# TensorE's loop over single batches with register addresses, and GpSimd instead of SyncE as the engine that opens and closes the section

## The chip, the cores and the metric

One core of one Trainium2 chip. The metric is the device time of one execution in microseconds; lower is better. The span of a profile runs from the first to the last instruction and is about 2.1 us shorter than the time. "The fifteenth" and "the sixteenth" below are DMA engines in the order in which they finish their share of a transfer. A landing is the moment at which such a share has arrived. A turn is the place in the queue where a store follows loads; a long load packet is one that took more than the usual 1.82 us.

## The reference

```python
batch, m, k, n = 16, 512, 768, 1024          # x: [16, 768, 512], y: [16, 768, 1024], float32
def reference(x, y):
    return np.einsum('bkm,bkn->bmn', x, y).astype(np.float32)
```

## The kernel before

SyncE issues all transfers on one queue. VectorE casts x and y of a batch to bf16, GpSimd turns the casts into counts for TensorE, TensorE does 48 matmuls of 128x128 by 128x512 per batch into two PSUM tensors, ScalarE copies each half out, and a store of 2 MiB follows. The program has buffers for the loads of two batches and for five outputs.

```python
ctx.enter_context(tc.tile_critical())                      # SyncE opens and closes
xb = [ec(nc.sbuf_tensor(f"xb{i}", [P, KT, M], BF16)) for i in range(2)]
yb = [ec(nc.sbuf_tensor(f"yb{i}", [P, KT, N], BF16)) for i in range(2)]
# ...
def parts(b):                                              # y is cast in two parts in these batches
    return 2 if b in (0, 1, 2, 14, 15) else 1
# ...
for b in range(B):                                         # SyncE
    if b >= 2: nc.sync.wait_ge(cast, nx[b - 2])
    wide_dma("x", ...)                                     # 1.5 MiB
    if b >= 2: nc.sync.wait_ge(cast, nx[b - 2] + parts(b - 2))
    wide_dma("y", ...)                                     # 3 MiB
    if b >= LAG: store(b - LAG)                            # 2 MiB, LAG = 4
for b in range(B - LAG, B):
    store(b)
# ...
def batch(i):                                              # TensorE; i is a Python constant
    # ...
    nc.tensor.wait_ge(ready, 2).then_inc(ready, -2)
    for g in range(2):
        nc.tensor.wait_ge(room, 1).then_inc(room, -1)
        for m in range(HB):
            for nt in range(NT):
                for kt in range(KT):
                    if g == 0 and m == 0 and nt == 0 and kt == KH:
                        nc.tensor.wait_ge(ready, 1).then_inc(ready, -1)
                    mm = nc.tensor.matmul(ps[g][:, m, nt], x_w[:, kt, g * HB + m],
                                          yb[i][:, kt, nt * NF:(nt + 1) * NF], ...)
        mm.then_inc(groups, 1)

with nc.Fori(0, B // 2, engines=OrderedEngineSet([pe])):   # a hardware loop, two batches each
    batch(0)
    batch(1)
```

## Time and profile before

| | before |
|---|---|
| time, median of 3 runs | 262.86 us (262.63 to 263.0) |
| span of the profile | 260.7 us |
| DMA queue busy, share of 16 engines | 97.9% |
| TensorE busy | 72%, granted clock 0.91 |
| packets of kind "instruction" | 1, of 16,384 bytes |

The page and the answers of the profile on which the argument rests are in the prediction below. Beside them it uses the trace's records of single DMA packets (start, duration, size) and of landings. The trace has 16 landings for each of the 48 transfers (768), one from each of the 16 DMA engines, and whoever waits for a transfer waits for the last of them: of the last y the fifteenth landed at 233.15 us and the sixteenth at 235.23, and its cast began at 235.26. The packet of 16,384 bytes of kind "instruction" is called the fetch below.

### The profile page before, as it was taken

The numbers are of one execution on the slowest core, as the hardware profiler recorded it, in microseconds if no ns is written. First come the engines' busy times: TensorE is split into PE (matmuls) and PEld (weight loads), VectorE is DVE, ScalarE is ACT, GpSimd is POOL, SyncE is SP. The second block draws the span as 40 slices with busy tenths as digits, with TensorE's granted clock in tenths as the row PEclk, the third lists the DMA queues.
The fourth block names the chain that finished last, engine by engine and source line by source line (L and its number), as shares of the span: only waits on it lengthen the run. The fifth ranks groups of instructions, "written<-read, shape, count | busy, mean of one in ns | idle before, by whom it ended". The sixth has DMA issues, their size and how long they took to land. (4 is left out here: it accounts for less than half of the span.)

```text
span 260.7 us, 1850 instructions
## 1 busy us (share of the span) xinstructions
PE 188.3 (72%) x760; PEld 88.9 (34%) x768; DVE 82.3 (32%) x37; ACT 61.1 (23%) x33; POOL 0.2 (0%) x4
## 2 busy tenths in 40 slices
PE   0049999797955949779695894969869196895930
PEld 0014555343522514324242341434334043341510
DVE  0271743425213252322524114252132523225000
ACT  1001322414230220402223022130412214022220
POOL 0000000000000000000000000000000000000000
PEclk9999999999997997959899796797999889797995
DMA  7998999989999999999999989999898999989984
GB/s 272 422 513 370 475 387 453 430 334 460 425 417 463 400 450 460 420 407 415 473 407 430 473 375 468 392 480 430 380 493 380 470 437 435 422 385 432 435 359 209
DMA packets 4513, 109.07 MB, mean 418 GB/s; under 512 B 768, under 2 KB 768, under 8 KB 768
## 3 DMA queue, kind: packets, MB, share of 16 engines
q1 hardware_dynamic: 4512, 109.05, 97.9%
q8 instruction: 1, 0.02, 0.0%
HBM read 75.50 MB, written 33.55 MB: 418 GB/s over the span
## 5 line engine op out<-in xcount | busy, mean ns | idle before, releaser
L143 PE MATMUL ps<-yb,xb 128*128 128x512 bf16 x760 | 188.3, 410 | 61.4 <-PEq L137 59.3
L143 PEld LDWEIGHTS ps<-yb,xb 128*128 128x128 bf16 x768 | 88.9, 117 | 160.4 <-issue 95.0
L161 ACT COPY ob<-ps 128x2048 f32<-128x2048 f32 x32 | 59.8, 1869 | 189.6 <-PE ps L143 189.6
L124 DVE CAST yb<-ys 128x6144 bf16<-128x6144 f32 (+1 forms) x21 | 54.1, 2596 | 88.0 <-DMA ys<-in_y_dram 88.0
L120 DVE CAST xb<-xs 128x3072 bf16<-128x3072 f32 x16 | 28.2, 1760 | 68.4 <-DMA xs<-in_x_dram 67.2
L161 ACT ACT_TABLE_LOAD x1 | 1.3, 1283 | 1.0 <-SPq L45 1.0
L185 POOL MEMSET const-bfloat16-1.0<- 128x1 bf16 x1 | 0.1, 102 | 0.0
L185 POOL MEMSET const-uint8-127<- 128x1 uint8 x1 | 0.1, 101 | 0.0
L185 POOL MEMSET const-float32-0.0<- 128x1 f32 x1 | 0.1, 99 | 0.2 <-issue 0.2
L185 POOL MEMSET const-float32-1.0<- 128x1 f32 x1 | 0.1, 98 | 0.0
## 6 DMA issues: line engine op xcount, KB each, us to landing
ys<-in_y_dram SPq DMA_DIRECT2D x16, 3072.0 KB, 28.2
out_dram<-ob SPq DMA_DIRECT2D x16, 2048.0 KB, 32.6
xs<-in_x_dram SPq DMA_DIRECT2D x16, 1536.0 KB, 29.7
```

Source lines behind the costliest of these rows:

```text
L120: nc.vector.tensor_copy(xb[i][:], xs[i][:]).then_inc(cast, 1)
L124: nc.vector.tensor_copy(yb[i][:, ks], ys[i][:, ks]).then_inc(cast, 1)
L143: mm = nc.tensor.matmul(ps[g][:, m, nt], x_w[:, kt, g * HB + m], yb[i][:, kt, nt * NF:(nt + 1) * NF], start=(kt == 0), stop=(kt == KT - 1))
L161: cp = nc.scalar.copy(ob[b % NO][:, g * HB:(g + 1) * HB].rearrange("p m (t f) -> p m t f", f=NF), ps[g][:])
L185: nc = _bacc.Bacc("TRN2", target_bir_lowering=False, num_devices=1)
```

## The change

TensorE's loop runs over single batches, an inner hardware loop gives the slot (0 or 1) as a register, and the operands' addresses are computed from it. For that the two slots of xb and yb become one tile each. The order becomes kt outside nt. y is cast in two parts in the last batch only. GpSimd opens and closes the section and waits for the stores at the end. The intent, as far as the code tells it: a shorter program, on TensorE above all.

```diff
-    ctx.enter_context(tc.tile_critical())
+    ctx.enter_context(tc.tile_critical(sync_engine=nc.gpsimd.engine))
-    xb = [ec(nc.sbuf_tensor(f"xb{i}", [P, KT, M], BF16)) for i in range(2)]
-    yb = [ec(nc.sbuf_tensor(f"yb{i}", [P, KT, N], BF16)) for i in range(2)]
+    xb = ec(nc.sbuf_tensor("xb", [P, 2, KT, M], BF16))
+    yb = ec(nc.sbuf_tensor("yb", [P, 2, KT, N], BF16))
     ... (VectorE's casts write xb[:, i] and yb[:, i, ks] accordingly)
-        return 2 if b in (0, 1, 2, 14, 15) else 1
+        return 2 if b in (15,) else 1
-    def batch(i): ... (above)
-    with nc.Fori(0, B // 2, engines=OrderedEngineSet([pe])):
-        batch(0)
-        batch(1)
+    x_w = xb[:].rearrange("p s k (j mo) -> p s k mo j", mo=MT)
+    pe = OrderedEngineSet([nc.tensor.engine])
+    with nc.Fori(0, B // 2, engines=pe):
+        with nc.Fori(0, 2, engines=pe) as s:
+            nc.tensor.wait_ge(ready, 2).then_inc(ready, -2)
+            for mo in range(MT):
+                g, m = divmod(mo, HB)
+                if m == 0:
+                    nc.tensor.wait_ge(room, 1).then_inc(room, -1)
+                for kt in range(KT):
+                    if mo == 0 and kt == KH:
+                        nc.tensor.wait_ge(ready, 1).then_inc(ready, -1)
+                    for nt in range(NT):
+                        mm = nc.tensor.matmul(
+                            ps[g][:, m, nt], x_w[:, bass.ds(s, 1), kt, mo],
+                            yb[:, bass.ds(s, 1), kt, nt * NF:(nt + 1) * NF],
+                            start=(kt == 0), stop=(kt == KT - 1))
+                if m == HB - 1:
+                    mm.then_inc(groups, 1)
     for i in range(NO):
-        nc.sync.wait_ge(so[i], 16 * len(range(i, B, NO)))
+        nc.gpsimd.wait_ge(so[i], 16 * len(range(i, B, NO)))
```

More of the change, by code (lines that the diff above doesn't have):

```diff
@@ L119 @@
         nc.vector.wait_ge(sx[i], n)
-        nc.vector.tensor_copy(xb[i][:], xs[i][:]).then_inc(cast, 1)
+        nc.vector.tensor_copy(xb[:, i], xs[i][:]).then_inc(cast, 1)
         nc.vector.wait_ge(sy[i], n)
@@ L123 @@
             ks = slice(h * KT // parts(b), (h + 1) * KT // parts(b))
-            nc.vector.tensor_copy(yb[i][:, ks], ys[i][:, ks]).then_inc(cast, 1)
+            nc.vector.tensor_copy(yb[:, i, ks], ys[i][:, ks]).then_inc(cast, 1)
     for b in range(B):
@@ L130 @@
             nc.gpsimd.wait_ge(cast, nx[b] + h + 1).then_inc(ready, 2 // parts(b))
-    def batch(i):
-        x_w = xb[i][:].rearrange("p k (j mo) -> p k mo j", mo=MT)
-        nc.tensor.wait_ge(ready, 2).then_inc(ready, -2)
-        for g in range(2):
-            nc.tensor.wait_ge(room, 1).then_inc(room, -1)
-            for m in range(HB):
-                for nt in range(NT):
-                    for kt in range(KT):
-                        if g == 0 and m == 0 and nt == 0 and kt == KH:
-                            nc.tensor.wait_ge(ready, 1).then_inc(ready, -1)
+    x_w = xb[:].rearrange("p s k (j mo) -> p s k mo j", mo=MT)
[11 more added lines that the diff above has]
+                    for nt in range(NT):
                         mm = nc.tensor.matmul(
-                            ps[g][:, m, nt], x_w[:, kt, g * HB + m],
-                            yb[i][:, kt, nt * NF:(nt + 1) * NF],
+                            ps[g][:, m, nt], x_w[:, bass.ds(s, 1), kt, mo],
+                            yb[:, bass.ds(s, 1), kt, nt * NF:(nt + 1) * NF],
                             start=(kt == 0), stop=(kt == KT - 1))
-            mm.then_inc(groups, 1)
-    pe = nc.tensor.engine
-    with nc.Fori(0, B // 2, engines=OrderedEngineSet([pe])):
-        batch(0)
-        batch(1)
+                if m == HB - 1:
+                    mm.then_inc(groups, 1)
     nc.scalar.nop().then_inc(room, 2)
```

## The prediction

Passages are cut from the prediction, and each cut is marked. The register work in TensorE's last batch was taken as hidden, so it entered the sum as 0. Expecting the shorter loop body, 133 instructions for 202, to end the fetch was the assumption; "If so" refers to it.

Three things in the prediction need their numbers from the trace. The branch quoted at 208 ns is the COMPARE_BRANCH of the lines below it. A "warm clock" stands for stretches with a matmul every 216 ns (at 36.4 us), as against every 427 ns (at 19.3 us); the granted clock was 0.50 in a stretch of the second kind at 80.5 to 83.5 us, but 1.00 in both at 19.3 and 36.4 us, so it doesn't explain the 427 ns at the start. And that the sequencer runs ahead of the array shows at the first jump: the branch is at 36.50 us, while ScalarE's copy, which waits for the last matmul of that body, began at 40.46.

> **What bounds the kernel now.** I read the page first, for which unit is full. The lines are busy time by engine, the DMA row of the 40 slices, and the queues.
>
> ```profile
> span 260.7 us, 1850 instructions
> PE 188.3 (72%) x760; PEld 88.9 (34%) x768; DVE 82.3 (32%) x37; ACT 61.1 (23%) x33; POOL 0.2 (0%) x4
> ...
> DMA  7998999989999999999999989999898999989984
> ...
> q1 hardware_dynamic: 4512, 109.05, 97.9%
> q8 instruction: 1, 0.02, 0.0%
> ```
>
> TensorE is busy 72% of the span, the 16 DMA engines 97.9%. One batch moves 1.5 + 3 + 2 MiB = 6.82 MB, and in the steady middle the casts of successive batches start 15.81 us apart (212.22 and 228.05 in the timeline), which is 431 GB/s. TensorE needs 10.5 to 13.4 us of the 15.81. So its loop has 2.4 to 5.3 us of slack per batch, and a change of TensorE's loop can reach the time only at the two ends, or through the DMA engines.
>
> Then the end, in the timeline, because the chain of waits shows only the last 13 us:
>
> ```profile
> 235.26 3.43 DVE L124 CAST yb<-ys 128x3072 bf16<-128x3072 f32 x2 [5.45 <-DMA ys<-in_y_dram]
> 237.37 0.59 PE L143 MATMUL ps<-yb,xb 128*128 128x512 bf16 x1 [2.73 <-PEq L137]
> ...
> 249.74 1.87 ACT L161 COPY ob<-ps 128x2048 f32<-128x2048 f32 x1 [3.25 <-PE ps L143]
> 251.63 0.33 SPq L98 DMA_DIRECT2D out_dram<-ob  x1
> ```
>
> The last y lands at 235.2, its first half is cast, TensorE works 12.4 us, ScalarE evicts, and the last store is issued at 251.63. One would say that this chain sets the end. But the waits of the DMA queue's engine say something else:
>
> ```profile
> SPq L45 <- DMA out_dram<-ob: 4.8, 1, 4.8
> SPq L170 <- DMA out_dram<-ob: 2.6, 1, 2.6
> ```
>
> After issuing the last store SyncE still waits 2.6 us for the store before it, and then 4.8 us for the last one; 4.8 us is just what one store takes on a full queue (8 packets of 16 KiB per DMA engine, 611 ns each in the packet records, 4.89 us). I therefore went through the landing records, 16 for each transfer, one per DMA engine. Up to the fifth transfer's landing at 36.4 us all 16 arrive within 0.7 us. From the transfer of 39.4 on, fifteen engines land together and one lands 1.45 us behind; from 58 us on it is 2.1 us behind, and stays so until the end (y of batch 15: fifteenth at 233.15, sixteenth at 235.23; the store before the last: 252.85 and 254.63). Semaphores wait for all 16, so **one late DMA engine sets the end**: it never gets a pause and finishes at 259.46, while the other fifteen stood idle near 252.5, waiting for the last store.
>
> What made it late is the one packet that isn't data: queue 8, kind instruction, 16,384 bytes, at 37.72 us, took 1,069 ns. It starts 1.0 us after TensorE's first jump back to the loop's start (branch at 36.50, 0.22 us long). The further 0.7 us is lost at 55.5 to 56 us, where the packets of all engines run long (2.3 to 3.1 us for 1.83).
>
> [...] this trace has 208 ns at the median on TensorE:
>
> ```profile
> L150 PEldq ALU_OP  x8: 36/36/42, 36.4 to 245.7; - x8
> L150 PEldq COMPARE_BRANCH  x8: 76/208/224, 36.5 to 245.8; - x8
> ```
>
> **The change, part by part.**
>
> Loop body. It was 96 matmuls, each with a weight load, 8 waits and 2 loop instructions: 202 instructions. It becomes 48 matmuls with weight loads, 30 fused register instructions, 4 waits and 3 loop instructions (the built program): 133. [...] If so, the packet at 37.7 us goes, and with it the 1.45 us and most of what followed. The end is then set by the other fifteen engines: fifteenth landing of the store before the last at 252.85, plus 4.89 for the last one, gives 257.74 in place of 259.46, a gain of 1.7 us.
>
> Register work. The 30 fused instructions carry 108 register operations per batch (54 for the first 12 matmuls, 54 for the other 36). Priced as separate ALU operations of 36 ns they are 3.9 us of sequencer per batch, [...] against 12.4 us for a batch of array time. [...] Going back, the order kt before nt puts six matmuls instead of three before the wait for the second half of y, which is worth the 0.2 us that TensorE stood still at 237.96.
>
> Does that reach the end? If the late engine is cured, the last y lands 2.1 us earlier (233.15), so the last store could be issued at 249.5, while fifteen engines are busy with the store before it until 252.85. In the old trace the last store needed 6.26 us from issue to its fifteenth landing (251.63 to 257.89), so the compute path alone would end at 255.8, and TensorE has about 1.9 us to give before it is felt. [...]
>
> Casts in one part (batches 0, 1, 2, 14). TensorE starts batches 0 to 2 up to 1.7 us later, one half cast. The x cast of batch 2 waits for the end of batch 0, so its load of batch 4 is issued about 1 us later, but that load has over 10 us of others queued ahead of it. Nothing is lost. Batch 14 ends at 236.2 instead of 234.5, before batch 15 can start at 237.4. Its store comes 1.7 us later, into a queue that still holds three stores. Nothing.
>
> Opening and closing by GpSimd. The first load waits for another engine's signal: before, it was issued at 0.95 us with SyncE's own at 0.7. I allow 0.1 us at the start. At the end GpSimd takes over five waits that came to 1.2 us from the last landing to the end of the span with SyncE: 0.1 us more.
>
> Sum: -1.7 + 0.2 = -1.5 us if the fetch goes, about +0.2 if it stays.
>
> **Rivals.** (1) The fetch stays, because it belongs to the backward jump and not to the length of the code; the nested loop has more jumps. For it: the packet follows the first jump by 1.0 us. Against: seven jumps were taken and one packet came. Time then 262.9 us, or 263.5 with a second fetch on the same DMA engine. (2) The register work costs more than I priced, since a matmul with a register address may be decoded slowly. Up to 1.9 us per batch nothing shows; a batch of 15.8 us of TensorE time instead of 12.4 would make it the bound and cost 1 us at the end and then some per batch. For it: no number in the trace; against: the sequencer runs ahead of a 216 ns array, and only one register instruction stands per pair in three quarters of the loop. (3) The late engine is replaced by another loss, like the one at 55.5 us, which I can't explain: 262 us.
>
> **Range and chances.** I give 0.6 to the fetch going with hidden register work (262.86 - 1.5 = 261.4 us), 0.28 to the first rival and the third (262 to 263.5), 0.12 to the second (263 upwards, in a small part over 268). Two per cent is 5.3 us; DMA bytes are unchanged and bound the kernel, so faster by that is nearly excluded: 0.02. Slower by over 2%: 0.05. Within: 0.93. Predicted 261.4 us, range 260.5 to 263.3.
>
> **What would show it.** Right: no instruction packet during the loads and stores, all 16 landings of every transfer within some 1.5 us, the last landing 1.7 us earlier in the span[...]. Wrong: a 16 KiB instruction packet anywhere before 240 us and one engine late ever after; or matmuls of the later three quarters of a batch spaced by more than 216 ns with a warm clock, which would make the register work real; or a first load later than 1.1 us.

## The result, and the profile after

| | before | after |
|---|---|---|
| time, median, first comparison (4 runs each) | 262.93 us | 262.51 us (262.22 to 262.81) |
| ratio, 95% interval | | 0.9982 (0.996 to 1.0003) |
| time, median, second comparison (9 and 5 runs) | 262.89 us | 262.24 us (262.11 to 262.52) |
| ratio, 95% interval | | 0.9979 (0.9966 to 0.9993) |
| span of the profile | 260.7 us | 260.1 us |

A ratio is the mean time of one kernel's runs over that of the other's runs of the same rounds, so it is not quite the ratio of the medians quoted. The first comparison alone doesn't separate the two; the second, in five rounds on one chip, does: the medians differ by 0.42 and 0.65 us, and the second interval allows 0.2 to 0.9. 1.5 us were forecast, in the right direction and more than twice too large.

The page of the kernel after, the lines that answer to those of before:

```profile
span 260.1 us, 2388 instructions
PE 186.5 (72%) x768; PEld 89.9 (35%) x768; DVE 82.0 (32%) x33; ACT 61.1 (23%) x33; POOL 0.2 (0%) x4
...
DMA  7998999999999999999999999999999999989995
...
q1 hardware_dynamic: 4512, 109.05, 98.3%
HBM read 75.50 MB, written 33.55 MB: 419 GB/s over the span
```

The line of the instruction queue is gone: the one fetch of 16 KiB no longer happens. The data bytes are the same, and the DMA engines are even a little fuller (98.3% for 97.9%).

The price of the register addresses, from the instructions of the matmul line of the kernel after (count, durations in ns: shortest, median, longest):

```profile
L146 PE MATMUL ps<-yb,xb x768: 379/379/634, 18.3 to 248.7; 128*128 x192
L146 PEldq FUSED_REGOPS  x480: 46/46/83, 18.2 to 244.7; - x160
```

A fused register instruction took 46 ns, 30 of them 1.4 us per batch, where I had 3.9 us from separate operations. The timelines of a batch that ran wholly at the narrow spacing (a matmul every 216 ns and none at 427), before and then after (start, length, how many, idle before it and the releaser), show that nothing of it reaches the array:

```profile
191.51 10.53 PE L143 MATMUL ps<-yb,xb 128*128 128x512 bf16 x48 [3.58 <-PEq L137]
```

```profile
175.16 10.55 PE L146 MATMUL ps<-yb,xb 128*128 x48 [3.56 <-PEq L141]
```

48 matmuls in 10.53 and in 10.55 us: with 0.38 us for the last one that is 216 ns from start to start in both.

The start and the end of the kernel after, in its timeline:

```profile
0.89 0.39 SPq L71 DMA_DIRECT2D xs<-in_x_dram  x1
...
234.53 3.43 DVE L124 CAST yb<-ys 128x3072 bf16<-128x3072 f32 x2 [5.46 <-DMA ys<-in_y_dram]
236.86 1.01 PEld L146 LDWEIGHTS ps<-yb,xb 128*128 x6 [4.14 <-issue]
236.87 12.26 PE L146 MATMUL ps<-yb,xb 128*128 x48 [3.67 <-PEq L141]
...
249.16 1.87 ACT L160 COPY ob<-ps 128x2048 f32<-128x2048 f32 x1 [3.26 <-PE ps L146]
251.05 0.33 SPq L98 DMA_DIRECT2D out_dram<-ob  x1
```

TensorE's last batch takes as long as before (12.3 us), the wait for the second half of y no longer interrupts it, and the last store is issued 0.58 us earlier. The last y landed 0.72 us earlier (234.51 for 235.23), where I had expected 2.1. So the compute path didn't lose the gain; the DMA engines never gave it.

The landings of the store before the last, in us, and the last landing of all:

```
             first     fifteenth   sixteenth   last landing of the kernel
before       251.40     252.85      254.63        259.46
after        251.54     253.90      253.92        258.75
```

The late engine is gone: the sixteenth follows the fifteenth by 0.02 us. But the fifteenth itself is 1.05 us later than it was. Its place was the base of my sum.

Where the others lost it is in the packet records. A load packet of 48 KiB takes 1.82 us. From 60 us on I added up what packets took beyond that (those over by more than 0.03 us, all 16 engines together): 0.6 us before, 8.0 us after. In the kernel after, the landings of a transfer lie 1.0 us apart at 80 us, 1.6 us at 115, 2.3 us at 155, and from there stay at 2.2 to 2.4 us to the end. Most of the long packets there (19 of the 27 that were over by more than 0.1 us) start less than 1 us before some engine begins a store packet.

That is enough to account for the places. From the transfer that landed at 67 us to the store before the last, the mean of the 16 landings fell back by 0.40 us against the kernel before (from 0.08 us earlier to 0.32 later); the 7.4 us more in long packets are 0.46 us for each of 16 engines, an estimate from the two sums. What was lost before 60 us is not in these sums: at the first turn, in packets that start at about 55.5 us, it was 12.4 us before and 13.8 after.

### The profile page after: what moved, and what is told of

It is laid out like the page before. It is cut to its first block, busy times and chain, and to the rows that moved or that the text cites. A ratio compares the mean times of both kernels' runs of the same rounds, so it can differ in the third digit from the quotient of the medians.

```text
span 260.1 us, 2388 instructions
## 1 busy us (share of the span) xinstructions
PE 186.5 (72%) x768; PEld 89.9 (35%) x768; DVE 82.0 (32%) x33; ACT 61.1 (23%) x33; POOL 0.2 (0%) x4
## 3 DMA queue, kind: packets, MB, share of 16 engines
q1 hardware_dynamic: 4512, 109.05, 98.3%
## 5 line engine op out<-in xcount | busy, mean ns | idle before, releaser
L146 PE MATMUL ps<-yb,xb 128*128 x768 | 186.5, 408 | 62.7 <-PEq L141 62.7
L146 PEld LDWEIGHTS ps<-yb,xb 128*128 x768 | 89.9, 117 | 158.7 <-issue 92.2
```

Source lines behind the costliest of these rows:

```text
L146: mm = nc.tensor.matmul(ps[g][:, m, nt], x_w[:, bass.ds(s, 1), kt, mo], yb[:, bass.ds(s, 1), kt, nt * NF:(nt + 1) * NF], start=(kt == 0), ...
```

## The experiments

The theory: (T) the length of TensorE's code draws the fetch, and the fetch makes one DMA engine late for good. On the missing gain there were three: (A) how much the other engines lose is chance from one execution to the next; (B) an engine that is late keeps the others from losing time; (C) something in the new code slows them.

### The two kernels again

`before_again` and `after_again` are unchanged copies.

> The kernel before, unchanged, for a second set of landing records. Every theory: one 16 KiB instruction packet about 1.0 us after TensorE's first backward jump (36.5 us), one DMA engine 1.4 to 2.2 us behind ever after. On the missing gain: if the fifteen other engines' lateness is chance (theory A), the fifteenth landing of the store before the last may lie anywhere from 252.8 to 254.0 us; if they are early because one engine is late (theory B) or because this code is kinder to them (theory C), it is again within 0.3 us of 252.85.

> The changed kernel, unchanged, timed in five rounds. Every theory: no instruction packet, all 16 landings of a transfer close on each other's heels (sixteenth at most 0.3 us after fifteenth); time 0.3 to 0.8 us under before. Theory A: the fifteenth landing of the store before the last lies anywhere from 252.8 to 254.0 us. Theories B and C: again 253.9 within 0.3 us.

Measured: before_again 262.98 us (one run), the packet of 16 KiB at 37.76 us, the fifteenth of the store before the last at 252.79. after_again 262.24 us, no packet, the last at 253.92 as in the first execution, but the fifteenth at 253.50: 0.42 us before the sixteenth, where at most 0.3 had been expected, and 0.1 us outside what B and C had said. So the two kernels differ as they had, and neither is a whim of one profile, but single places vary by some 0.4 us from one execution to the next.

### The addresses alone undone

```diff
-        with nc.Fori(0, 2, engines=pe) as s:
+        for s in range(2):
   ... x_w[:, s, kt, mo], yb[:, s, kt, nt * NF:(nt + 1) * NF]
```

> The changed kernel with the register addresses alone undone: two batches with constant addresses per loop iteration, so the loop body is again 202 instructions for TensorE; everything else (order of kt and nt, one tile for both slots, casts, GpSimd as opener) as changed. Theory of length: the instruction packet is back at 37 to 40 us and one engine 1.4 to 2.2 us behind; time within 0.3 us of before. Rival, that the jump or the register loop as such matters: no packet. On the missing gain: theory B (the late engine relieves the others): fifteenth landing of the store before the last back at 252.85 within 0.3; theory C (the merged tiles, casts or opener slow the others): it stays at 253.9.

> The kernel with constant addresses again (late engine by the fetch). First time it lost 6.3 us in long load packets, as much as the kernels without a late engine, but its fifteen others stayed within 1.7 us. Theory B (a late engine keeps the others from losing): under 3 us this time and the others within 1.5 us. Chance: anything from 0.6 to 7 us.

Measured: 263.06 us for 262.89 of before in five rounds, ratio 1.0006 (0.9992 to 1.0019). The page has the fetch again:

```profile
span 261.0 us, 1852 instructions
...
q1 hardware_dynamic: 4512, 109.05, 97.9%
q8 instruction: 1, 0.02, 0.0%
q14 instruction: 1, 0.00, 0.0%
```

(The packet of q8 at 39.57 us in the first execution, 37.77 in the second. The one of q14 has 32 bytes and stands at 0.07 us, before the first load; it has no part in this.) The last engine is 3.4 to 3.5 us behind the first, as in the kernel before. Here GpSimd, the casts, the merged tiles and the order kt before nt are all as changed, and with the fetch back they show no gain together (the interval is -0.2 to +0.5 us); the gain goes with the register loop. The fifteenth is at 253.07, within B's range and against C; the second time at 253.17, 1.76 us behind the first engine, where B had said at most 1.5. In long load packets this kernel lost 6.3 us the first time (most of it in a burst at 126 to 136 us) and 2.8 the second (263.15 us, one run), where B had said under 3.

### The code made longer again, with nothing else changed

```diff
+    for _ in range(72):                      # pad36: 36
+        nc.tensor.nop().then_inc(pads, 1)
     pe = OrderedEngineSet([nc.tensor.engine])
```

> The changed kernel with 72 semaphore increments on TensorE put ahead of its loop, where it waits for the first 18 us anyway; loop, jumps and addresses unchanged. Theory of length: the code up to the loop's end is again as long as before's, so one instruction packet comes as TensorE first reaches the end of the body, at about 27 to 29 us (first batch), and one engine is 1.4 to 2.2 us behind from the next transfer on; time 0.2 to 0.7 us over the changed kernel. Rival (the fetch belongs to the form of the loop): no packet, time as the changed kernel's within 0.2 us.

> The padded kernel again (late engine by the fetch). First time 1.7 us lost, others within 1.7 us. Theory B: under 3 us, others within 1.8 us of the first engine at the store before the last. Chance: anything from 0.6 to 7 us.

> The changed kernel with 36 increments on TensorE ahead of the loop in place of 72, to bracket the length at which the fetch comes: a packet if the limit lies between 36 and 0 instructions above the changed kernel's body end, none if it lies between 36 and 66 above. No theory forecasts which. With a packet one engine is 1.4 to 2.4 us late and the time is 262.8 to 263.2; without, 262.0 to 262.5.

Measured: pad72 263.05 us, ratio to before 1.0005 (0.9991 to 1.0019); to the changed kernel in the same rounds 0.8 us more. The fetch is back, at 30.3 us in both executions, a batch earlier than before since the loop's end is now reached after one batch (first jump at 27.43 us). I had said 27 to 29 us; it came 1.2 us after the jump in the kernel before and 2.9 us here. In all six executions with a fetch the packet begins within 3 to 4 ns of the end of a load packet (37.721 and 37.724 us in the kernel before, where the load packets beside it start 3 to 4 ns before the end of another), which speaks for its waiting its turn on a DMA engine. One engine is 1.4 us late from the next transfer on. The padding itself ran from 1.0 to 11.9 us, while TensorE had nothing to do:

```profile
L136 PEldq EVENT_SEMAPHORE  x72: 51/51/51, 1.0 to 11.9; - x72
```

The queues on the page of pad72 and then of pad36:

```profile
q1 hardware_dynamic: 4512, 109.05, 97.9%
q8 instruction: 1, 0.02, 0.0%
```

```profile
q1 hardware_dynamic: 4512, 109.05, 98.1%
```

pad36 has no fetch (262.70 us, one run; above the 262.0 to 262.5 that I expected). So T holds: the form of the loop is the same in all three and only the length differs. TensorE's own instructions up to the end of the loop body may be about 170 (133 and 36) and not about 205 (133 and 72); the rival that the fetch belongs to the backward jump is refuted, since the changed kernel jumps and fetches nothing.

### The loop alone

The kernel before with TensorE's loop and the merged tiles of the change; SyncE and the casts as before.

> The kernel before with the TensorE part of the change alone (one batch per iteration by register addresses, kt before nt, the two slots in one tile); SyncE opens and closes, casts in two parts for batches 0, 1, 2, 14, 15 as before. Theory: no instruction packet, time as the changed kernel's, 0.5 to 0.8 us under before. Rival (the other two parts carry some of the gain): within 0.3 us of before. Theory B (a late engine relieves the others): without it, the last landing of the store before the last is at 253.9 within 0.3 us again, and the mean of its 16 landings at 252.3 or later.

Measured: 262.53 us (261.96 to 263.09), ratio 0.9989 (0.9975 to 1.0003), no fetch, last engine at 253.88, mean of the 16 landings 252.49. The times scatter too much to separate the loop from the whole change or from before, but the records are those of the changed kernel.

### A late engine without a fetch

```diff
+    scratch = ec(nc.sbuf_tensor("scratch", [17, 512], FP32))
     for b in range(B):                       # ScalarE
         ... copies of batch b
+        if b == 1:
+            nc.scalar.dma_start(scratch[:], x[0, 0:17, :]).then_inc(extra, 16)
```

The reasons for this load, and for the one of the next section, to run on a single engine are cut. What the packets and landings showed is given with each result.

> The changed kernel plus one small load of 17 rows of 2 KB into a scratch tile nobody reads, issued by ScalarE after batch 1 (about 41 us)[...]. Theory of the late engine: what counts is not that it was code but that one engine lost 1 to 1.5 us: one engine 1.4 to 2.4 us behind for the rest, time up by 0.4 to 0.9 us over the changed kernel. Theory B: the fifteen others at the store before the last come back from 253.5 to 253.9 to 253.1 or less. Rival (only instruction fetches do this, or a spread of 2.4 us is reached anyway): fifteenth landing stays at 253.5 to 253.9, time within 0.2 us of the changed kernel.

> The kernel with the implanted load again (late engine without a fetch). First time 3.5 us lost and the fifteenth engine 2.5 us behind the first. Theory B: under 3 us and fifteenth within 1.8 us. Chance, or a spread that grows anyway: fifteenth again over 2 us behind. Every theory: last engine 3.0 to 3.5 us behind the first, time 262.7 to 263.2.

Measured: 263.02 us, ratio to before 1.0003 (0.9989 to 1.0016). So it isn't the fetch as such: other work that makes one engine late cost the whole gain here too. But the fifteenth came at 253.95, 2.5 us behind the first (2.1 the second time), with 3.5 and 4.4 us lost in long packets. That was a miss for B. One thing differs from the fetch, though: the 17 small packets (84 to 89 ns each, from 46.6 to 64.3 us) took turns with the data, and the sixteenth landing fell behind the fifteenth bit by bit, 0.1 us at the transfer that landed at 51.3 us, 0.6 at 59.7, 1.8 at 76.8: only in part before the first store, whose packets start at about 57.9 us.

### The late engine before the first store

```diff
-    scratch = [17, 512], load of x[0, 0:17, :] after batch 1
+    scratch = [1, 4099], one load of 4,099 contiguous numbers after ScalarE's first copy   # implant_early
+    scratch = [4, 4099], four such loads at the same place                                # implant_four
```

> The changed kernel with one load of 4,099 contiguous numbers (16 KB[...]) from ScalarE's queue after its first copy, about 27 us: one packet of the size of an instruction fetch, on one DMA engine, before the first store is in the queue at 55 us. Theory B2 (an engine that is late before the first turn from loads to stores keeps the rest from losing time): last engine 3.1 to 3.5 us, fifteenth at most 1.8 us behind the first at the store before the last, under 3 us lost in long load packets, time 262.7 to 263.2. Rival (it needs the instruction fetch, or chance): fifteenth 2.0 us or more behind as with the first implant; time the same 262.7 to 263.2, since the late engine sets it either way.

> The same kernel a second time, since the packet records differ from run to run: same expectations as for the first.

Measured: 262.68 us (262.28 to 263.12), ratio 0.9995 (0.9973 to 1.0016). The packet was there (616 ns, at 30.0 us), but it fell on the engine that was earliest, and no engine was late afterwards. So it didn't test what it was for. Nor does its time separate from that of the kernel before. It counts as two more executions with no late engine: 8.8 and 9.9 us lost in long packets, last engine 2.7 us behind.

> The single implanted packet took 616 ns and fell on the engine that was earliest, so no engine became late. Now four such packets at the same place (about 2.5 us on one engine, 0.6 of which it was early): one engine should be 1.5 to 2.2 us behind the others from 40 us on, before the first store. Theory B2 (such an engine keeps the rest from losing time): at the store before the last the fifteenth at most 1.8 us, the last 3.0 us or more behind the first, under 3 us lost in long load packets. Rival: fifteenth 1.9 us or more behind, 5 us or more lost in long load packets.

> The kernel with four implanted packets a second time, because the packet records differ from one execution to the next; the same expectations as for the first: fifteenth at most 1.8 us behind and under 3 us lost by theory B2, 1.9 us or more and 5 us or more by the rival.

Theory B2 in these expectations is B with one condition more: the engine has to be late before the first store. Measured: 263.7 us each (one run each; before beside them 263.06). One engine is 1.9 to 2.1 us behind the next at the transfer that lands at 52.9 us. At the store before the last the fifteenth is 1.66 and 1.85 us behind the first, the last 3.85 and 3.93; 0.95 and 1.54 us are lost in long packets. All as B2 says but for 0.05 us in the second fifteenth, and against the rival on each point. (The four packets cost one engine more than the fetch did, and the time is 0.6 us over before's.)

### Half as many turns from loads to stores

```diff
-        if b >= LAG:
-            store(b - LAG)
+        if b > LAG and b % 2 == 1:
+            store(b - LAG - 1)
+            store(b - LAG)
```

> The changed kernel with stores issued two and two, every second batch, so that the queue turns from loads to stores half as often. If the engines lose their time at the turn from loads to stores (the long load packets stand just before a store), the spread of the 16 landings at the end falls from 2.4 us to under 2, and the time drops by 0.3 to 0.8 us under the changed kernel; this would be the version that beats both. If the losses don't belong to the turns: time within 0.3 us of the changed kernel. It may also be slower if a copy has to wait for its output buffer (the trace would show ScalarE waiting for a store).

Measured: 262.30 us, ratio to before 0.9978 (0.9964 to 0.9991); beside loop_only, not beside the changed kernel, whose ratio to before is 0.9979. So it beats before but not the change, and the expected further gain isn't there. The cause is split: fifteen engines now stay within 1.0 us of each other to the end, and long load packets all but vanish after the first turn (1.5 us after 70 us). Fewer turns do keep the engines together. But one engine lost about 0.1 us with each store (1.8 us over the 16, if it is the same one throughout), in store packets of mostly 615 to 634 ns for 611, and ended 2.6 us behind. It is no peculiarity of this kernel: if each packet is put behind the one at whose end it starts, which gives 16 chains, every one of the 18 executions has one engine whose packets in the last five stores take 0.25 to 0.46 us more in all than 611 ns each (0.35 before, 0.41 after, 0.36 here). In the kernels before and after it isn't the last one; here and in loop_only it is. Why one engine stores more slowly is open.

### All packet records side by side

Behind the first engine at the store before the last, in us, and the time lost in long load packets after 60 us (paired: after 70):

| kernel | fetch | an engine late before the first store | lost in long load packets | fifteenth | sixteenth | last landing |
|---|---|---|---|---|---|---|
| before | yes | yes | 0.6 | 1.45 | 3.23 | 259.46 |
| before_again | yes | yes | 1.7 | 1.45 | 3.40 | 259.56 |
| static_two | yes | yes | 6.3 | 1.68 | 3.46 | 259.68 |
| static_again | yes | yes | 2.8 | 1.76 | 3.40 | 259.64 |
| pad72 | yes | yes | 1.7 | 1.72 | 3.51 | 259.56 |
| pad72_again | yes | yes | 1.8 | 1.71 | 3.19 | 259.30 |
| implant_four | no | yes | 1.0 | 1.66 | 3.85 | 259.91 |
| implant_four2 | no | yes | 1.5 | 1.85 | 3.93 | 260.11 |
| implant | no | partly | 3.5 | 2.52 | 3.32 | 259.50 |
| implant_again | no | partly | 4.4 | 2.08 | 3.12 | 259.54 |
| after | no | no | 8.0 | 2.36 | 2.38 | 258.75 |
| after_again | no | no | 7.3 | 2.13 | 2.54 | 258.74 |
| after_third | no | no | 6.3 | 2.53 | 2.82 | 259.04 |
| loop_only | no | no | 5.9 | 2.18 | 2.30 | 258.72 |
| pad36 | no | no | 6.8 | 2.47 | 2.86 | 259.22 |
| implant_early | no | no | 8.8 | 1.94 | 2.67 | 259.10 |
| implant_early2 | no | no | 9.9 | 2.01 | 2.66 | 258.97 |
| paired | no | no | 1.5 | 1.01 | 2.56 | 258.78 |

> A third set of packet records of the changed kernel, to tell chance from a rule. Kernels with no late engine have so far lost 5.9 to 8.0 us in all over the 16 engines in long load packets after 60 us, with the last engine 2.3 to 2.9 us behind the first at the store before the last. Both theories: again 5.5 us or more, and 2.2 us or more.

after_third: as expected in both numbers. Its time of 262.55 us (one run) shows no gain, since before took 262.60 beside it (one run, on another chip than that of the five rounds); one run of each settles nothing about a difference of 0.6 us.

Read by groups: in the eight executions with an engine late before the first store the fifteenth is 1.45 to 1.85 us behind, and seven of them lose under 3 us. In the seven without a late engine (paired left out) nothing is under 5.9 us, and the sixteenth is 2.3 to 2.9 us behind. Against A: the places don't overlap between the groups, and the losses in one execution only.

## Why the prediction was wrong

**What it had right.** One late DMA engine sets the end before; an instruction fetch made it late; a shorter loop body ends the fetch; jumps don't draw it (24 loop branches in the trace of the kernel after, and no fetch). The bound stays the DMA engines. The register work is hidden, and cheaper than I had it (1.4 us of sequencer per batch, not 3.9). The casts in one part cost nothing, and batch 14 ended before batch 15 could start. The wait that TensorE met in the last batch is gone. At the start I had expected 0.1 us more and the first load was issued 0.06 us earlier (0.89 for 0.95); at the end the time from the last landing to the end of the span went from 1.24 to 1.30 us, where I had said 0.1 more. Together about nothing.

Some of the working was off without bearing on the result: it calls the landing at 36.4 us that of the fifth transfer, but it is the sixth; the two casts shown at 212.22 and 228.05 us are 15.83 us apart, not 15.81; and batch 14 ended earlier (233.2 us), not 1.7 us later.

**The step that failed** is the sentence "The end is then set by the other fifteen engines: fifteenth landing of the store before the last at 252.85, plus 4.89 for the last one, gives 257.74 in place of 259.46, a gain of 1.7 us." The second addend held (4.83 us in the kernel after, 253.92 to 258.75). The first didn't: without the late engine the last of the engines was at 253.92. The term of the sum measured -0.7 us, not -1.7. One of the prediction's own signs of being right failed with it: the 16 landings were to stay within some 1.5 us of each other, and from 91 us on most transfers took longer, 2.4 us at the end. Its third rival, "the late engine is replaced by another loss, like the one at 55.5 us", with 262 us, is what came.

I had taken the places of fifteen engines from a run in which the sixteenth was late, as if they didn't depend on it. They do: given an engine late before the first store, with or without a fetch, the engines lost 0.6 to 2.8 us in long load packets (6.3 us once); without one they lost 5.9 to 9.9 us (paired, with half the turns, 1.5 after 70 us), and the last among them lands 1.0 to 1.6 us later than the old fifteenth. So about 1 us of the 1.7 us was given back in longer load packets of the other engines. The mean of all 16 landings of the store before the last shows the same: 252.14 us before, 252.46 after, though one engine had been cured of 1.45 us. That the late engine makes the difference rests on putting one there in several ways (static_two, pad72, implant_four) and taking it away; implant, late only in part at the first store, lost an amount between those of the two groups.

**What stays open.** Why a late engine spares the others. The long packets stand at the turns from loads to stores (load packets of 1.82 us took up to 1.99 us before and 2.51 after from 60 us on, and 2.2 to 3.1 us in both at the first turn, 55.5 us), and fewer turns keep the engines closer (paired); that is what the records show, and no run shows the mechanism behind it. One rival is untested: casts and issues wait for the sixteenth landing, so a late engine also moves them against the others' packets (a y load is issued at 80.52 us before and at 78.67 after, while the first landing of the store next to it is at 79.19 and 79.15). Its plain forms find little support: of the 27 packets in the kernel after that were over by more than 0.1 us, none overlaps a cast by VectorE and two an issue by SyncE; 14 overlap a copy by ScalarE, but in the kernel before such copies fill 0.8 us or more of the last 2 us ahead of seven turns without one packet that long. Nor is it known why static_two lost 6.3 us once with its others still within 1.7 us. The loss of all engines at 55.5 us, in both kernels, belongs to the first turn: in paired, which has no store there, the packets that start at 55.4 to 56.1 us took 1.83 us each, and the long ones (up to 2.5 us) came at 66.4 to 67.1 us, before its first store at 68.5.

## What to carry to other kernels

Where DMA engines are full and whoever waits for a transfer waits for its last share, look at the landings engine by engine: one stray packet of 16 KiB on one engine, 38 us into the kernel, set the end 220 us later here, though it is 0.02 MB of 109. TensorE's own lines don't show it: in the kernel before its matmuls ran on without a pause from 16.57 to 50.78 us. When you remove such a straggler, don't take the second-latest of the old run as the new last: the others' places were measured with the straggler there, and the gain read off them here was 1.7 us for 0.7 measured. A few instructions more or less can be worth more by what they fetch than by what they take: the 72 of pad72 ran while TensorE had nothing to do, and cost 0.8 us.
